# Reordering the first loads, the squares and the warm-up matmuls in the opening of a hybrid attention block

## The chip, the cores and the metric

The kernel runs on one core of one Trainium2 chip. The metric is the device time of one execution in microseconds (us), lower is better; a version's time is the median of its runs.

## The reference

The block normalises `x` (512 tokens of 2048 features, float32), multiplies it with a wide input weight, runs two groups of attention heads on the result, multiplies with an output weight, adds `x` and normalises again. What matters here is only its first step:

```python
y = xf * lax.rsqrt(jnp.mean(xf * xf, axis=-1, keepdims=True) + RMS_EPS)
h = y * norm_g
proj = h @ w_in[l]
```

The rest (rotary positions, compressed, selected and windowed attention of group A, windowed attention with sinks of group B, the gates and the output product) is not touched by the change.

## The kernel before

The kernel holds `x` transposed: 16 tiles of 128 features by 512 tokens, indexed by `k`. Products run in three matmuls of rounded words (`mm3`, lines 118 to 121): every operand is split in a high word (`xh`, `whi`), which is the operand rounded, and a low word (`xl`, `wlo`), which is what is left. Line 119 multiplies high by high, line 120 low `x` by high weight, line 121 high `x` by low weight.

The opening is the loop of lines 178 to 188 over `k`. For each `k` it loads one tile of `x` (`load_x`, 256 KB) and one tile of the first 512 weight columns (`w0`, 256 KB), splits both, and issues 4 times 3 matmuls of 128 x 512 into four accumulators. The division by the root of the mean square is not done here: the loop also sums the squares of `x` over the 16 tiles in `sqa`, and lines 190 to 198 turn the sum into the scale `rstdb` that later results are multiplied with. `norm_g` does enter here. It lies in the small tile `gt` (128 rows of 17 numbers, 8.5 KB), and ScalarE multiplies by a column of it while it rounds:

```python
nc.sync.dma_start(xr, xT[:, k, :])
last["xh"] = act.activation(xh[:, k, :], xr, AF.Copy, scale=gt[:, k:k + 1]).ins
```

So the first `xh` needs both the first tile of `x` and `gt`. VectorE then computes `xl` (`split_x`, line 153), also with `gt`. ScalarE squares the tile (lines 157 and 161), and GpSimd adds the square to `sqa` (line 162). The weights are rounded by ScalarE (line 97) and their rests taken by VectorE (line 99); for the first weight tile VectorE does both (lines 94 and 99).

Loads go through queues, each served in order: SyncE's (SP) has `gt` and then, in turns, tiles of `x` and of weights; ScalarE's (ACT) has only the first weight tile (line 92 with `opening=True`). Tiles of `x` have 5 buffers (`tmp`, line 142), raw weights 3, split weights 3, and the square 1.

Before the loop, `WARM` = 40 matmuls of a 128 x 128 tile of zeros with itself run on TensorE (lines 175 and 176). They produce nothing that is used.

The program is written in a framework that sets the semaphores itself and orders the instructions of each engine by a planner; `tc.issue_after(i)` forces an instruction behind `i` on the same engine.

Of the kernel before, what the change touches and what calls it, by code (L numbers as in the profile page):

```python
# [10 lines left out]
F32 = mybir.dt.float32  # L11
F32R = mybir.dt.float32r
AF = mybir.ActivationFunctionType
# [4 lines left out]
P = 128  # L18
S = 512
# [7 lines left out]
SCALE_B = 64 ** -0.5  # L27
CMP = 32
MOVING, EVEN, STILL, BELOW = 0, 16, 32, 48
WARM = 40  # L30
ORDER = [0, 1, 2, 3, 4, 5, 8, 9, 10, 11, 6, 7, 12, 13, 14, 15]
TAB_W = 512 + NQ * CMP + 256

# [2 lines left out]
def hybrid_block(ctx, tc, xT, xtm, w0, wv0, wv1, wz, wq, wo0, wos, cw1, cw2, cpos, e2, rope, tabs, sinks, gT, fg, out):  # L36
    nc = tc.nc
    pe, act, dve, pool = nc.tensor, nc.scalar, nc.vector, nc.gpsimd

    def sb(name, bufs=1, side=None):  # L40
        return tc.tile_pool(name=name, bufs=bufs, side=side)
# [13 lines left out]
    gt = const.tile([P, KT + 1], F32, name="gt")  # L55
# [13 lines left out]
    last = {}  # L69
# [6 lines left out]
    def raw():  # L76
        raws[0] += 1
        return weights(f"raw{raws[0] % 3}")

    def words(place):  # L80
        return [wp.tile([P, 1088], F32R, name=nm, tag=nm)[:, place:place + 1024] for nm in ("whi", "wlo")]
# [6 lines left out]
    def load_unit(src, width, opening=False, place=EVEN, after=None, after_lo=None, loaded=None):  # L88
        rw = loaded or raw()
        hi, lo = words(place)  # L90
        if loaded is None:
            last["dma"] = (nc.scalar if opening else nc.sync).dma_start(rw[:, :width], src).ins
        if opening:
            dve.tensor_copy(hi[:, :width], rw[:, :width])
        else:
            with tc.issue_after(after) if after else nullcontext():
                last["hi"] = act.activation(hi[:, :width], rw[:, :width], AF.Copy).ins  # L97
        with tc.issue_after(after_lo) if after_lo else nullcontext():
            last["lo"] = dve.tensor_tensor(out=lo[:, :width], in0=rw[:, :width], in1=hi[:, :width].bitcast(F32),  # L99
                                           op=ALU.subtract).ins  # L100
        return hi, lo
# [6 lines left out]
    xh = xpool.tile([P, KT, S], F32R, name="xh")  # L108
# [9 lines left out]
    def mm3(ps, ah, al, bh, bl, first, last, go_on=False):  # L118
        pe.matmul(ps, ah, bh, start=first, stop=False, skip_group_check=go_on)  # L119
        pe.matmul(ps, ah, bl, start=False, stop=False, skip_group_check=go_on)  # L120
        recent["mm"] = pe.matmul(ps, al, bh, start=False, stop=last, skip_group_check=go_on).ins  # L121
# [15 lines left out]
    s0b = p0.enter_context(sb("s0b", bufs=2))  # L137
# [1 line left out]
    ps0 = p0.enter_context(tc.tile_pool(name="ps0", bufs=1, space=PSUM))  # L139

    def tmp(name):
        return s0b.tile([P, S], F32, name=name, tag="tmp", bufs=5)

    def load_x(k):
        xr = tmp("xr")
        if k == 0:
            nc.sync.dma_start(gt, gT)
        nc.sync.dma_start(xr, xT[:, k, :])
        last["xh"] = act.activation(xh[:, k, :], xr, AF.Copy, scale=gt[:, k:k + 1]).ins
        return xr  # L150

    def split_x(k, xr):
        dve.scalar_tensor_tensor(out=xl[:, k, :], in0=xr, scalar=gt[:, k:k + 1], in1=xh[:, k, :].bitcast(F32),
                                 op0=ALU.mult, op1=ALU.subtract)
        if k == 0:
            with tc.issue_after(last["xh"]):
                act.activation(sqa, xr, AF.Square)
        else:
            sq = s0b.tile([P, S], F32, name="sq", tag="sq", bufs=1)
            with tc.issue_after(last["xh"]):  # L160
                act.activation(sq, xr, AF.Square)
            pool.tensor_tensor(out=sqa, in0=sqa, in1=sq, op=ALU.add)

    def bank(i):
        if i >= 6:
            return psp.tile([P, 512], F32, name="pj", tag="pj")
        return ps0.tile([P, 512], F32, name=f"bank{i}", tag=f"bank{i}")

    sqa = s0.tile([P, S], F32, name="sqa", tag="sqa")
# [4 lines left out]
    idle = bank(0)  # L174
    for i in range(WARM):
        pe.matmul(idle[:, 0:P], still, still, start=True, stop=True)
    acc0 = [bank(i) for i in (4, 2, 5, 3)]
    for k in range(KT):
        if k == 0:
            hi, lo = load_unit(w0[:, 0, 0:512], 512, opening=True)  # L180
            xr = load_x(k)
        else:
            xr = load_x(k)
            hi, lo = load_unit(w0[:, k // 2, (k % 2) * 512:(k % 2) * 512 + 512], 512)
        split_x(k, xr)
        for i in range(4):
            o = i * P
            mm3(acc0[i], hi[:, o:o + P], lo[:, o:o + P], xh[:, k, :], xl[:, k, :], k == 0, k == KT - 1)
# [220 lines left out]
    def rows(m):  # L409
        if m < 6:  # L410
            xr = rb.tile([P, 2, S], F32, name="rows", tag="rows")
        else:
            xr = wk.tile([P, 2, S], F32, name="rows", tag="raw3", bufs=1)
        with tc.issue_after(last["dma"]):
            nc.sync.dma_start(xr, xT[:, 2 * m:2 * m + 2, :])
        return xr
# [46 lines left out]
    xr = None  # L463
    for i in range(8):
# [4 lines left out]
        if 0 < i < 7:  # L469
            xr = rows(i - 1)  # L470
# [346 lines left out]
    xr = rows(6)  # L817
# [11 lines left out]
    for u in range(4):  # L829
# [10 lines left out]
        if u == 0:  # L840
            build(6, xr)
            xr = rows(7)
# [308 lines left out]
    for c, u, ms in ((0, 0, ()), (0, 1, ()), (0, 2, ()), (1, 0, (0, 1, 2)), (1, 1, (3, 4)), (1, 2, (5, 6)), (0, 3, ()),  # L1151
                     (1, 3, (7,))):
        hi, lo = load_unit(wo0[:, c, u], 1024, place=MOVING, loaded=first_units.pop(0) if first_units else None, after=last["qh"],
                           after_lo=low_y[11] if (c, u) == (0, 2) else last["turn"])
# [365 lines left out]
```

## Time and profile before

| what | value |
|---|---|
| time, median of 3 runs | 802.83 us (802.57 to 803.43) |
| time of the profiled execution | 802.8 us |
| its span, first to last instruction | 801.0 us |
| TensorE (PE) busy | 789.6 us, 99% of the span |
| VectorE (DVE) busy | 686.3 us, 86% |
| ScalarE (ACT) busy | 504.7 us, 63% |
| GpSimd (POOL) busy | 108.3 us, 14% |
| granted TensorE clock, mean | 0.997 |

A profile shows one execution. PE is the row of matmuls, PEld that of their weight loads. Matmuls overlap, and the end of one is modelled, so the step from one start to the next is the real pace. "ACTq" and "SPq" are the queues that issue transfers.

### The profile page before, as it was taken

What the parts mean: (1) busy time and instruction counts of PE and PEld (TensorE: products, weight loads), DVE (VectorE), ACT (ScalarE), POOL (GpSimd) and SP (SyncE); (2) the same over time, 40 slices, a digit from 0 to 9 for tenths busy, and PEclk for the clock granted to TensorE, in tenths of its full rate; (3) what the DMA queues carried; (4) which work ended last, traced back from release to release, by engine and by line L of the source; (5) the groups of instructions that cost most, each with busy time, mean ns of one, the idle gap of its engine ahead of it and who ended that gap; (6) DMA issues with size and microseconds to landing.
All of it is one profiled execution on the core that took longest, in us unless ns stands there. A gap on an engine that the chain in (4) does not pass through costs nothing.

```text
span 801.0 us, 15316 instructions
## 1 busy us (share of the span) xinstructions
PE 789.6 (99%) x5693; PEld 739.1 (92%) x5693; DVE 686.3 (86%) x1407; ACT 504.7 (63%) x1103; POOL 108.3 (14%) x111
## 2 busy tenths in 40 slices
PE   9999999999999999999999999999999999999996
PEld 8788888888888899999999999999999999999996
DVE  7668988889989597759999999998999798978895
ACT  6646657655666356664447778777777867553545
POOL 3615002110121000323210110110100000000000
PEclk9999999999999999999999999999999999999998
DMA  7572243564373469887723213225216836797845
GB/s 239 172 242 81 79 144 106 171 171 150 101 210 106 158 200 281 257 269 194 207 82 106 68 53 119 82 92 159 71 50 216 296 120 219 257 266 193 258 86 211
DMA packets 49563, 131.05 MB, mean 164 GB/s; under 512 B 6000, under 2 KB 8848, under 8 KB 49488
## 3 DMA queue, kind: packets, MB, share of 16 engines
q1 hardware_dynamic: 43376, 110.89, 42.3%
q0 software_dynamic: 5824, 18.65, 10.5%
q8 instruction: 45, 0.74, 0.4%
q10 hardware_dynamic: 288, 0.52, 0.2%
q14 instruction: 30, 0.25, 0.1%
HBM read 113.23 MB, written 16.81 MB: 162 GB/s over the span
## 4 chain that ended last, share of the span: by engine, by line
PE 86%; DVE 6%; DMA 3%; ACT 2%; issue 2%; POOL 0%; SPq 0%; DVEq 0%; ACTq 0%
PE pj L119 16%; PE pj L121 15%; PE pj L120 15%; PE oa L120 5%; PE oa L119 5%; PE oa L121 5%; PE sp L932 4%; PE bank L121 2%; PE bank L120 2%; PE bank L119 2%; DMA xr<-xT 2%; DVE wlo L543 2%; PE tp L969 2%; PE tp L384 2%; DMA raw<-wq 1%
## 5 line engine op out<-in xcount | busy, mean ns | idle before, releaser
L119 PE MATMUL pj<-xh,whi 128*128 128x256 f32 (+1 forms) x592 | 196.9, 333 | 0.6 <-ACT t L608 0.5
L121 PE MATMUL pj<-xh,wlo 128*128 128x256 f32 (+1 forms) x592 | 196.2, 331 | 0.0
L120 PE MATMUL pj<-xl,whi 128*128 128x256 f32 (+1 forms) x592 | 196.1, 331 | 0.0
L119 PEld LDWEIGHTS pj<-xh,whi 128*128 128x128 f32 x592 | 111.4, 188 | 11.0 <-ACT t L608 0.9
L121 PEld LDWEIGHTS pj<-xh,wlo 128*128 128x128 f32 x592 | 111.4, 188 | 10.1
L120 PEld LDWEIGHTS pj<-xl,whi 128*128 128x128 f32 x592 | 111.4, 188 | 9.7
L543 DVE TENSOR_TENSOR wlo<-raw,whi 128x1024 fp32r<-128x1024 f32 (+2 forms) x80 | 92.9, 1172 | 7.8 <-ACT whi L542 7.2
L542 ACT ACTIVATE whi<-raw 128x1024 fp32r<-128x1024 f32 (+2 forms) x80 | 77.6, 985 | 30.7 <-DVE raw L581 11.5
L99 DVE TENSOR_TENSOR wlo<-raw,whi 128x1024 fp32r<-128x1024 f32 (+1 forms) x61 | 72.1, 1184 | 22.8 <-ACT whi L97 22.3
L97 ACT ACTIVATE whi<-raw 128x1024 fp32r<-128x1024 f32 (+1 forms) x60 | 56.6, 945 | 28.8 <-PE pj L120 14.8
L120 PE MATMUL oa<-wlo,xh 128*128 128x256 f32 x200 | 55.5, 278 | 0.0
L119 PE MATMUL oa<-whi,xh 128*128 128x256 f32 x200 | 55.4, 278 | 0.0
L121 PE MATMUL oa<-whi,xl 128*128 128x256 f32 x200 | 55.2, 276 | 0.0
L121 PE MATMUL pj<-pu,wlo 128*128 128x256 f32 x160 | 45.0, 281 | 0.5 <-DVE wlo L543 0.5
L119 PE MATMUL pj<-pu,whi 128*128 128x256 f32 x160 | 45.1, 282 | 0.4 <-DVE zr L581 0.4
L120 PE MATMUL pj<-pu,whi 128*128 128x256 f32 x160 | 44.7, 279 | 0.0
L289 DVE TENSOR_TENSOR pl<-tp,ph 128x512 fp32r<-128x512 f32 (+1 forms) x64 | 40.7, 651 | 3.1 <-ACT ph L288 2.9
L288 ACT ACTIVATE ph<-tp 128x512 fp32r<-128x512 f32 (+1 forms) x64 | 34.1, 560 | 9.6 <-PE tp L969 4.4
L363 ACT ACTIVATE ttb<-ttb,sums 128x256 f32<-128x256 f32 (+1 forms) x64 | 30.0, 471 | 14.4 <-DVE sums L356 14.4
L121 PEld LDWEIGHTS oa<-whi,xl 128*128 128x128 f32 x200 | 37.6, 188 | 0.0
L120 PEld LDWEIGHTS oa<-wlo,xh 128*128 128x128 f32 x200 | 37.6, 188 | 0.0
L119 PEld LDWEIGHTS oa<-whi,xh 128*128 128x128 f32 x200 | 37.5, 188 | 0.0
(401 smaller groups left out, 2369.8 us busy)
## 6 DMA issues: line engine op xcount, KB each, us to landing
raw<-wq SPq DMA_DIRECT2D x41, 512.0 KB, 4.4
raw<-wz SPq DMA_DIRECT2D x36, 512.0 KB, 4.0
cw<-cw SPq DMA_DIRECT2D x32, 256.0 KB, 4.0
raw<-wos SPq DMA_DIRECT2D x14, 512.0 KB, 5.9
rw<-wos SPq DMA_DIRECT2D x10, 512.0 KB, 4.8
xr<-xT SPq DMA_DIRECT2D x16, 256.0 KB, 3.4
rows<-xT SPq DMA_DIRECT2D x8, 512.0 KB, 4.7
raw<-wo SPq DMA_DIRECT2D x8, 512.0 KB, 6.0
```

The costliest lines, as they stand in the source:

```text
L97: last["hi"] = act.activation(hi[:, :width], rw[:, :width], AF.Copy).ins
L99: last["lo"] = dve.tensor_tensor(out=lo[:, :width], in0=rw[:, :width], in1=hi[:, :width].bitcast(F32), op=ALU.subtract).ins
L119: pe.matmul(ps, ah, bh, start=first, stop=False, skip_group_check=go_on)
L120: pe.matmul(ps, ah, bl, start=False, stop=False, skip_group_check=go_on)
L121: recent["mm"] = pe.matmul(ps, al, bh, start=False, stop=last, skip_group_check=go_on).ins
L288: act.activation(ph, tp, AF.Copy)
L289: dve.tensor_tensor(out=pl, in0=tp, in1=ph.bitcast(F32), op=ALU.subtract)
L363: act.activation(tv, tv, AF.Exp, bias=mn[:, e, v:v + 1], scale=-1.0, accum_out=dn[:, e, v:v + 1])
L384: pe.transpose(tp[:, o:o + P], tts[kt + s][:, v, c0:c0 + P], ident)
L542: split_hi = act.activation(hi, src, AF.Copy).ins
L543: last["lo"] = dve.tensor_tensor(out=lo, in0=src, in1=hi.bitcast(F32), op=ALU.subtract).ins
L932: pe.matmul(sp[:, a:b], qq[:, qs], kk[:, ko:ko + b - a], start=pi == 0, stop=pi == 2)
```

## The change

It touches the opening alone. `gt` leaves SP's queue and is issued on ACT's queue, behind the first weight tile; so the first tile of `x` is the first entry of SP's queue. The square and its addition leave `split_x` for a function of their own, `add_square`; the squares of tiles 0, 1 and 2 are issued later, in the turns of `k` = 2 and 3 (tile 0 at 2; 1 and 2 at 3; 3 and 4 at 4; from 5 on each in its own turn), and behind a rounding of weights on ACT. The square has two buffers and the tiles of `x` six. The matmuls on zeros are 33, where there were 40.

```diff
-WARM = 40
+WARM = 33
...
-        return s0b.tile([P, S], F32, name=name, tag="tmp", bufs=5)
+        return s0b.tile([P, S], F32, name=name, tag="tmp", bufs=6)
 
     def load_x(k):
         xr = tmp("xr")
-        if k == 0:
-            nc.sync.dma_start(gt, gT)
         nc.sync.dma_start(xr, xT[:, k, :])
         last["xh"] = act.activation(xh[:, k, :], xr, AF.Copy, scale=gt[:, k:k + 1]).ins
         return xr
...
-        if k == 0:
-            with tc.issue_after(last["xh"]):
-                act.activation(sqa, xr, AF.Square)
-        else:
-            sq = s0b.tile([P, S], F32, name="sq", tag="sq", bufs=1)
-            with tc.issue_after(last["xh"]):
-                act.activation(sq, xr, AF.Square)
+
+    def add_square(k, xr):
+        sq = sqa if k == 0 else s0b.tile([P, S], F32, name="sq", tag="sq", bufs=2)
+        with tc.issue_after(last["xh"]), tc.issue_after(last["hi"]) if k < 3 else nullcontext():
+            act.activation(sq, xr, AF.Square)
+        if k:
             pool.tensor_tensor(out=sqa, in0=sqa, in1=sq, op=ALU.add)
...
+    behind = []
     for k in range(KT):
         if k == 0:
             hi, lo = load_unit(w0[:, 0, 0:512], 512, opening=True)
+            nc.scalar.dma_start(gt, gT)
             xr = load_x(k)
         else:
             xr = load_x(k)
             hi, lo = load_unit(w0[:, k // 2, (k % 2) * 512:(k % 2) * 512 + 512], 512)
         split_x(k, xr)
+        behind.append((k, xr))
+        for late in range(k >= 2 and min(len(behind), 1 + (k > 2))):
+            add_square(*behind.pop(0))
```

## Rows read from the trace of the kernel before

**Rows 1.** Busy time by engine: us, share, instructions.

```profile
PE 789.6 (99%) x5693; PEld 739.1 (92%) x5693; DVE 686.3 (86%) x1407; ACT 504.7 (63%) x1103; POOL 108.3 (14%) x111
```

**Rows 2.** What PE waited for: total us, times, longest.

```profile
PE bank L176 <- DVE still L173: 1.2, 1, 1.2
PE tp L457 <- issue: 0.6, 1, 0.6
```

**Rows 3.** PE in order of time, opening: start, us, instruction.

```profile
1.16 4.07 PE L176 MATMUL bank<-still 128*128 128x128 bf16 x40 [1.16 <-DVE still L173]
5.09 1.19 PE L119 MATMUL bank<-xh,whi 128*128 128x512 f32 x4
6.12 0.39 PE L120 MATMUL bank<-xl,whi 128*128 128x512 f32 x1
```

**Rows 4.** Stretches, matmuls on zeros: length, busy (x running), clock, DMA, GB/s.

```profile
2.42:3.49 1.07, 1.07 (x13) 1.00 0.99 346
...
4.70:5.00 0.30, 0.30 (x8) 1.00 0.97 335
```

**Rows 5.** ACT and its queue in order of time, opening.

```profile
0.73 0.40 ACTq L92 DMA_DIRECT2D raw<-w  x1
1.17 1.28 ACT L67 ACT_TABLE_LOAD   x1 [1.17 <-PEq L1511]
...
4.32 0.72 ACT L149 ACTIVATE xh<-xr,gt 128x512 fp32r<-128x512 f32 x1 [1.65 <-DMA xr<-xT]
...
6.89 0.62 ACT L97 ACTIVATE whi<-raw 128x512 fp32r<-128x512 f32 x1
```

**Rows 6.** DVE in order of time, around the first `xl`.

```profile
5.07 0.75 DVE L153 SCALAR_TENSOR_TENSOR xl<-xr,gt,xh 128x512 fp32r<-128x512 f32 x1 [0.33 <-ACT xh L149]
```

**Rows 7.** SP's queue in order of time, opening.

```profile
0.74 0.38 SPq L147 DMA_DIRECT2D gt<-gT  x1
1.17 0.89 SPq L148 DMA_DIRECT2D xr<-xT  x2
```

**Rows 8.** First transfers: queue, size, us from issue to landing.

```profile
raw<-w ACTq DMA_DIRECT2D x1, 256.0 KB, 2.8
gt<-gT SPq DMA_DIRECT2D x1, 8.5 KB, 2.5
...
xr<-xT SPq DMA_DIRECT2D x1, 256.0 KB, 3.1
```

**Rows 9.** Packets by queue from 2.3 to 2.6 us (q10 ACT's, q1 SP's): packets, MB, share.

```profile
q10 hardware_dynamic: 39, 0.08, 87.5%
q1 hardware_dynamic: 34, 0.00, 7.8%
```

**Rows 10.** One stretch, all engines: busy (x running), clock, DMA share, GB/s.

```profile
6.00:7.00 1.00, 1.00 (x6) 0.82 (x5) 0.50 (x1) 1.00 (x3) 0.00 (x0) 1.00 1.06 385
```

**Rows 11.** PE in order of time, 35 to 37 us.

```profile
35.63 0.39 PE L119 MATMUL bank<-xh,whi 128*128 128x512 f32 x1
36.33 0.50 PE L121 MATMUL bank<-xh,wlo 128*128 128x512 f32 x1 [0.31 <-DVE wlo L99]
36.67 0.40 PE L120 MATMUL bank<-xl,whi 128*128 128x512 f32 x1
```

**Rows 12.** ACT in order of time, 31 to 36 us.

```profile
32.35 0.72 ACT L149 ACTIVATE xh<-xr,gt 128x512 fp32r<-128x512 f32 x1 [0.16 <-DMA xr<-xT]
33.72 0.63 ACT L161 ACTIVATE sq<-xr 128x512 f32<-128x512 f32 x1 [0.64 <-POOL sqa L162]
34.26 0.61 ACT L97 ACTIVATE whi<-raw 128x512 fp32r<-128x512 f32 x1
```

**Rows 13.** DVE in order of time, the same stretch.

```profile
34.90 1.38 DVE L99 TENSOR_TENSOR wlo<-raw,whi 128x512 fp32r<-128x512 f32 x1 [0.67 <-ACT whi L97]
```

**Rows 14.** The last addition on POOL.

```profile
42.90 1.29 POOL L162 TENSOR_TENSOR sqa<-sqa,sq 128x512 f32<-128x512 f32 x1 [0.74 <-ACT sq L161]
```

**Rows 15.** PE's first use of the sum.

```profile
49.43 1.02 PE L191 MATMUL bank<-sqa,ones 128*128 128x512 f32 x2
```

**Rows 16.** Stretches at the end, all engines: columns as in Rows 10.

```profile
793.00:795.00 2.00, 0.45 (x4) 0.25 (x3) 0.62 (x3) 0.80 (x3) 0.00 (x0) 1.00 0.60 226
...
796.00:797.00 1.00, 0.00 (x0) 0.00 (x0) 0.21 (x1) 0.40 (x1) 0.00 (x0) 0.79 0.58 217
```

## The prediction

> **What bounds the kernel now.** I read the busy table first, then what PE waited for, then the opening engine by engine, and last the packets of its first transfers. The busy table leaves one candidate: PE works 789.6 of 801.0 us [rows 1]. The reader should see in the list of PE's waits how little is left: 1.2 us before its first instruction, and nothing else above 0.6 us [rows 2]. After the last matmul the span has only some 7.6 us of tail, from 793.45 on [rows 16]. So a microsecond by which the first real matmul moves passes through to the end nearly whole, and nothing that the change does on another engine counts unless PE gets its operands earlier or later for it. The change can therefore be priced at two places: where the real matmuls start, and where PE stands still inside the opening loop.
>
> The start. The matmuls on zeros run from 1.16 us, the first real matmul starts at 5.09 [rows 3]. In a stretch of 1.07 us there are 13 of the small ones, three of them overlapping neighbours of the stretch: one per 107 ns, which is 128 columns at 1.2 GHz; at 4.70 to 5.00 the pace is 56 ns, which is 2.4 GHz [rows 4]. The clock column reads 1.00 in both, so in this opening the spacing has to be read, not the column. The rise lies near 4.69 us, after 3.5 us of unbroken work. Forty in this pace end at 5.07. The first `xh` is ready at 4.32 + 0.72 = 5.04 [rows 5]. PE starts 0.05 later. Both conditions are met almost together: shortening the warm-up alone, or hastening `xh` alone, would give nothing.
>
> What makes `xh` late is its wait for the tile of `x`, which lands at 1.17 + 3.1 = 4.27 [rows 7, 8]; `gt` was there at 0.74 + 2.5 = 3.24.
>
> The standstill. At 35.63 a matmul starts, the next at 36.33, the one after at 36.67 [rows 11]. The undisturbed step is (6.12 - 5.09) / 4 = 0.26 at worst [rows 3], and 0.23 in the rows just ahead; so the place costs 0.70 + 0.34 - 2 x 0.23 = 0.58 us. Its releaser is `wlo`, and behind that a square: ACT's square waited 0.64 us for POOL to free its one buffer, the rounding of weights stood behind it on ACT until 34.26, and DVE took 1.38 us for the rest, to 36.28 [rows 12, 13].
>
> **The change part by part.**
>
> *Matmuls on zeros, 40 to 33.* The seven that go are the last ones, at 56 ns: 0.4 us. Thirty-three end at 1.16 + 33 x 0.107 = 4.69. PE is free from there; this is worth something only if `xh` comes before 5.04. By itself: 0.
>
> *x's first tile leads SP's queue.* It is issued at 0.74, not at 1.17: 0.43 us earlier [rows 7]. Whether it lands earlier depends on the transfer engines, which all queues share. Before, three transfers passed first: weights and `x` of 256 KB each and the 8.5 KB of `gt`, the last landing at 4.27. The two big ones still have to pass together, and both are needed for the first matmul (`whi` comes of the weights). Sixteen engines at 385 GB/s [rows 10] pass a row of 2 KB in 85 ns; 128 rows of each make 8 rows an engine. Taking away `gt`'s 8 short rows, about 12 ns each by their share in [rows 9] (7.8% of 16 engines x 0.3 us over 34 packets = 11 ns), saves 0.1 us: `x` and the first weights land at about 4.17. The weights land later than their 0.73 + 2.8 = 3.53 of before [rows 5, 8], since they now alternate with `x`, but still before `xh` is needed. The optimistic bound is the whole 0.43 us, `x` at 3.84.
>
> *gt behind the first weights.* This is where I expect the cost. `gt` now stands behind the weights in ACT's queue, and while it passes, SP's queue offers the second tile of `x`. How the engines share two queues is shown by the same two transfers of before: from 2.3 to 2.6 us, 39 packets of 2 KB of one queue and 34 short ones of the other passed [rows 9], so they take turns row by row. That is why 8.5 KB took 2.5 us to land beside 256 KB that took 2.8 [rows 8]. After the change, 8 rows of `gt` and its closing packet each wait for one row of 85 ns of `x`'s second tile: 9 x 85 + 8 x 12 = 0.86 us after 4.17, so `gt` lands at about 5.03. Then `xh` from 5.08 to 5.80, first matmul at about 5.85: 0.76 us later than before. The lower bound, if the short rows pass in one go, is 4.17 + 0.1 = 4.27, as `x` before: 0. I take 0.75, since rows 9 show exactly such a pair.
>
> The Trainium skill (DMA: Bandwidth & Descriptors, Queues, rings and completion order) says that an engine goes round the queues packet by packet and drains a whole packet of many descriptors, typically 9 to 17, before it switches. By that the eight rows of `gt` would pass in one turn and the sum would lose its 0.75; the counts of [rows 9] speak against it, one short packet for one long one.
>
> The issue itself costs ACT about 0.40 us, like the one at 0.73 [rows 5]; the table load behind it then ends near 2.85, not 2.45, and ACT is idle until `x` lands. Cost 0.
>
> *First L120.* `xl` takes 0.75 us behind `xh` [rows 6], and is needed 1.03 us after the first matmul [rows 3]: unchanged relative to the start, 0.
>
> *Squares of tiles 0 to 2 later, two buffers, six tiles of x.* Two squares of 0.54 us each (33.72 to 34.26, [rows 12]) leave ACT ahead of the rounding at 6.89, which ends at 7.51 [rows 5]. PE needs that for the second tile, twelve matmuls after its start: 5.09 + 1.03 + 8 x 0.23 = 7.96. It was in time already: 0. What counts is the second buffer: the square at 33.72 no longer waits 0.64 us, so `wlo` is there near 35.64 and the 0.58 us standstill goes. A start 0.75 later would by itself give the same slack: the two don't add. I take -0.58; the bound on the other side is 0, if another wait on DVE takes its place. The delayed squares need their additions on POOL done before PE reads the sum at 49.43; the last ended at 44.19 [rows 14, 15], a cover of 5.2 us. The delay is at the front, where POOL has time between turns: 15 additions of about 1.3 us are 20 us of work in a loop of 44: 0. If that cover went, PE would wait there for what is missing of it.
>
> *Sum.* +0.75 - 0.58 = +0.2 us (rounded) on the profiled execution's 802.8, which stands 0.03 below the median of its runs: 803.0. Bounds: start -0.43 to +0.76, standstill -0.58 to 0.
>
> **The rivals.**
>
> A, forecast: `gt` is the late operand and the standstill goes: 803.0, between 802.6 and 803.6 with the bound of the standstill.
>
> B: `gt` passes in one go; `xh` starts as before, the standstill goes: 802.8 - 0.6 = 802.2. For it: the page's rule. Against: rows 9.
>
> C, faster: `x` lands its whole 0.43 earlier with `gt` beside it. The first matmul comes at 4.66, just where 33 warm-up matmuls end: 802.8 - 0.43 - 0.58 = 801.8. For it: the fit with 33. Against: transfers that fill the engines, 385 GB/s a few us on. It decides if `xh` starts before 4.0.
>
> D, slower: the clock. In A, PE is idle from 4.69 to 5.85, around the moment at which it rose. If the rise is put off, the real matmuls run at 1.2 GHz, half pace. Let it need as much work again as before, 3.5 us from 5.85: half of it is lost, 1.75 us, giving 804.8. Against: at the end PE finishes at 793.45 and the clock column still averages 0.79 in 796 to 797, so it fell only near 796.6, after 3.1 us of rest [rows 16]; a gap of 1.2 need not do harm. For: rest before the rise is not shown by any row. It decides if the first real matmuls step by 0.43 us instead of 0.23.
>
> E: the planner orders instructions far behind the opening otherwise. No row speaks for a sign; either way, up to 2 us.
>
> **How the numbers follow.** A 0.50, B 0.24, C 0.07, D 0.13, E 0.06. From no change a measurement can tell about 0.2%, 1.6 us here: below 801.2 is faster, above 804.4 slower. A, B and C all lie inside. Slower is most of D and half of E with a little of A's tail, 0.15; faster is half of E and a little of C, 0.05; the same 0.80. The range takes A, B and C with the spread of runs, 801.7 to 804.2, and leaves out D and E.
>
> **What would show it.** In the profile after: `xr` landing near 4.2 and `gt` near 5.0; ACT's first `xh` waiting for `gt` and starting near 5.1; the first L119 near 5.85 and PE idle for about 1.1 us before it; no gap at the twelfth tile; squares that no longer wait for POOL for long; L191 about 0.2 us later than 49.43. I am wrong if `xh` starts by 4.4 (then B or C), if the first real matmuls step at half pace (D), or if PE's list of waits has a new entry above 0.5 us behind the opening (E).

## The result, and the profile after

The changed kernel takes 807.82 us (median of 11 runs), the kernel before 803.16 (11 runs beside them): a ratio of 1.0056, 95% interval 1.0042 to 1.0070, some 4.5 us slower. The forecast was 803.0 with a range of 801.7 to 804.2. The profiled execution took 808.47 us with a span of 806.7. One run of the kernel before, timed beside the experiments (983.27 us at a mean granted clock of 0.752), is in the slow state and left out of every ratio.

TensorE's list of waits now has two entries ahead of all others; its columns are those of [rows 2]. Lines 147, 151, 157, 159 and 173 of the changed kernel are lines 149, 153, 161, 162 and 176 of before.

```profile
PE bank L121 <- DVE wlo L99: 2.7, 3, 1.8
PE bank L119 <- ACT xh L147: 1.9, 1, 1.9
PE bank L173 <- DVE still L170: 1.2, 1, 1.2
```

The second entry is the start. PE in order of time, answering to [rows 3]:

```profile
1.16 3.31 PE L173 MATMUL bank<-still 128*128 128x128 bf16 x33 [1.16 <-DVE still L170]
6.36 1.30 PE L119 MATMUL bank<-xh,whi 128*128 128x512 f32 x4 [1.88 <-ACT xh L147]
7.46 0.63 PE L120 MATMUL bank<-xl,whi 128*128 128x512 f32 x1
...
8.31 0.63 PE L120 MATMUL bank<-xl,whi 128*128 128x512 f32 x1
8.74 0.63 PE L121 MATMUL bank<-xh,wlo 128*128 128x512 f32 x1
```

The first real matmul starts at 6.36, 1.27 us later than before, and from 7.46 on the step is 0.43 us: half pace. Why it starts late stands on ACT and its queue, answering to [rows 5], and in the first transfers, answering to [rows 8]:

```profile
1.23 0.39 ACTq L179 DMA_DIRECT2D gt<-gT  x1
2.46 0.20 ACT L67 ACTIVATE small<-small 128x1 f32<-128x1 f32 x1
5.58 1.33 ACT L147 ACTIVATE xh<-xr,gt 128x512 fp32r<-128x512 f32 x2 [2.92 <-DMA gt<-gT]
```

```profile
raw<-w ACTq DMA_DIRECT2D x1, 256.0 KB, 4.0
gt<-gT ACTq DMA_DIRECT2D x1, 8.5 KB, 4.3
...
xr<-xT SPq DMA_DIRECT2D x1, 256.0 KB, 3.8
```

ACT waits for `gt`, which lands at 1.23 + 4.3 = 5.5; the tile of `x` was there at 0.74 + 3.8 = 4.5 although it led its queue, 0.3 us later than the 4.27 of before. The packets from 4.2 to 4.8 us show `gt` (q10) among the tiles of `x` that follow the first (q1): 116 short packets beside 119, of which some 107 are rows of 2 KB (0.22 MB). Columns are as in [rows 9]:

```profile
q1 hardware_dynamic: 119, 0.22, 94.0%
q10 hardware_dynamic: 116, 0.01, 14.0%
```

The half pace is in the clock column this time (stretches of 1 us; columns as in [rows 10], the clock third from the end):

```profile
6.00:7.00 1.00, 0.64 (x3) 0.54 (x4) 0.66 (x1) 1.00 (x3) 0.00 (x0) 1.00 1.02 375
7.00:8.00 1.00, 1.00 (x5) 0.76 (x4) 1.00 (x3) 1.00 (x3) 0.00 (x0) 0.67 1.07 412
8.00:9.00 1.00, 1.00 (x4) 0.81 (x3) 1.00 (x3) 1.00 (x4) 0.00 (x0) 0.50 1.05 388
...
10.00:11.00 1.00, 1.00 (x4) 0.84 (x3) 1.00 (x2) 0.64 (x2) 0.00 (x0) 0.63 0.91 297
11.00:12.00 1.00, 1.00 (x6) 0.78 (x6) 0.80 (x2) 1.00 (x3) 0.08 (x1) 1.00 0.95 330
```

A mean of 0.67 in the second row puts the fall at 7.34, one of 0.63 in the fourth the rise at 10.74: 3.4 us in which a matmul steps by 0.43 and not 0.23, a loss of 3.4 x (1 - 0.227 / 0.427) = 1.6 us.

The first entry of the list is the larger surprise. The place answering to [rows 11], the largest of three:

```profile
33.87 0.39 PE L120 MATMUL bank<-xl,whi 128*128 128x512 f32 x1
36.09 0.73 PE L121 MATMUL bank<-xh,wlo 128*128 128x512 f32 x2 [1.84 <-DVE wlo L99]
```

The three cost 3.5 us together (steps of 0.65, 2.23 and 0.99 and the longer step of 0.335 behind each, less six of 0.227); before there was one of 0.58. VectorE and GpSimd around it, answering to [rows 13, 14]:

```profile
29.18 1.78 DVE L99 TENSOR_TENSOR wlo<-raw,whi 128x512 fp32r<-128x512 f32 x1
30.88 3.48 DVE L151 SCALAR_TENSOR_TENSOR xl<-xr,gt,xh 128x512 fp32r<-128x512 f32 x2
34.29 1.75 DVE L99 TENSOR_TENSOR wlo<-raw,whi 128x512 fp32r<-128x512 f32 x1
```

```profile
23.54 8.57 POOL L159 TENSOR_TENSOR sqa<-sqa,sq 128x512 f32<-128x512 f32 x5 [1.19 <-ACT sq L157]
32.46 4.73 POOL L159 TENSOR_TENSOR sqa<-sqa,sq 128x512 f32<-128x512 f32 x3 [0.35 <-ACT sq L157]
```

GpSimd adds without a pause, five additions in 8.57 us, and every VectorE operation beside it takes 1.75 us or so. The rounding of weights was done near 33.4; its `wlo` starts only at 34.29, behind two `xl`.

So the profile's 5.7 us are: start +1.27; half pace +1.6; standstills 3.5 - 0.58 = +2.9; together 5.8. PE's first use of the sum is at 55.28 (49.43 in [rows 15]), 5.85 later, and in this execution nothing more is lost behind the opening.

### The profile page after: what moved, and what is told of

It reads as the page before. It is cut to its first block, busy times and chain, and to the rows that moved or that the text cites. A ratio compares the mean times of both kernels' runs of the same rounds, so it can differ in the third digit from the quotient of the medians.

```text
span 806.7 us, 15317 instructions
## 1 busy us (share of the span) xinstructions
PE 791.9 (98%) x5686; PEld 739.6 (92%) x5686; DVE 690.5 (86%) x1407; ACT 505.0 (63%) x1103; POOL 110.7 (14%) x111
## 4 chain that ended last, share of the span: by engine, by line
PE 84%; DVE 8%; DMA 4%; issue 2%; ACT 2%; ACTq 0%; SPq 0%; DVEq 0%
PE pj L119 15%; PE pj L121 15%; PE pj L120 15%; PE oa L120 5%; PE oa L121 5%; PE oa L119 5%; PE sp L934 4%; PE bank L120 3%; PE bank L119 3%; PE bank L121 3%; PE tp L971 2%; DVE wlo L545 1%; PE tp L386 1%; DVE wlo L99 1%; DMA raw<-wq 1%
```

## The experiments

All were timed in five rounds beside the kernel before. Ratios are to before, with 95% intervals. "Start" is the first real matmul, "loop" the time from it to the first use of the sum; both are from PE's order of time in one profile each.

| kernel | ratio | interval | start us | loop us |
|---|---|---|---|---|
| before | 1 | | 5.09 | 44.34 |
| the change | 1.0056 | 1.0042 to 1.0070 | 6.36 | 48.92 |
| e1 gt alone | 1.0013 | 1.0001 to 1.0025 | 6.30 | 44.30 |
| e2 squares and buffers alone | 1.0056 | 1.0040 to 1.0071 | 5.39 | 49.81 |
| e3 change, gt put back | 1.0038 | 1.0025 to 1.0052 | 5.29 | 48.26 |
| e4 change, 60 on zeros | 1.0076 | 1.0060 to 1.0092 | 6.99 | 47.43 |
| e5 second square buffer alone | 1.0045 | 1.0029 to 1.0061 | 5.23 | 48.26 |
| e6 late squares alone | 1.0009 | 0.9996 to 1.0023 | 5.36 | 43.65 |
| e7 six buffers for x alone | 0.9999 | 0.9985 to 1.0013 | 5.37 | 44.26 |
| e8 as e2, additions on VectorE | 0.9989 | 0.9977 to 1.0000 | 5.37 | 43.72 |
| e9 change, additions on VectorE | 1.0005 | 0.9993 to 1.0018 | 6.39 | 45.26 |
| e10 as e9, gt second on SP | 0.9994 | 0.9980 to 1.0008 | 5.61 | 43.68 |
| e11 change, one square buffer | 1.0003 | 0.9991 to 1.0015 | 6.39 | 46.48 |
| e12 before, additions on VectorE | 1.0001 | 0.9987 to 1.0015 | 5.37 | 43.78 |

A profile is one execution. Behind the first use of the sum every version has the same matmuls, and yet this stretch took 751.6 us in the profile of before, 750.3 in that of e9 and 754.8 in that of e7. What a part costs is therefore read from the ratios, and that the parts of the change's profile add up to its span within 0.1 us is luck in part. Against the times expected, the medians of e2, e5, e10 and e12 came out 0.6 to 1.4 us above their ranges and that of e6 0.1 above; e3 came 1.0 us under e2, where 0.5 was allowed; e4 fell into its rival's range.

**e1: gt behind the first weights, nothing else.**

```diff
-        if k == 0:
-            nc.sync.dma_start(gt, gT)
...
             hi, lo = load_unit(w0[:, 0, 0:512], 512, opening=True)
+            nc.scalar.dma_start(gt, gT)
```

> The kernel before with one part of the change: gt leaves SP's queue and goes behind the first weights on ACT's; 40 matmuls on zeros, squares as before. Theory: the later landing of gt is the whole cause of the late start: gt lands near 5.5 us, first L119 at 6.3 to 6.4 us (5.09 before), the 40 matmuls on zeros end at 5.0 or, if the clock rises early, sooner, PE rests over 1 us, and the clock may or may not fall behind it; no standstill of more than 0.6 us near the twelfth tile. Time 0.8 to 2.5 us over before, 803.9 to 805.7. Rival: the squares carry most of the loss: then this is within 1 us of before.

The first real matmul starts at 6.30, and the loop is as long as before. ACT in order of time:

```profile
5.52 0.72 ACT L147 ACTIVATE xh<-xr,gt 128x512 fp32r<-128x512 f32 x1 [2.86 <-DMA gt<-gT]
```

The late start is wholly `gt`'s; its price is 0.13%, 1.0 us. The rest of 1.2 us before the first matmul did not bring the clock down in this profile. The time is also within the rival's 1 us: most of the loss lies elsewhere.

**e2: the squares and buffers, nothing else** (the changed kernel with `gt` as before and 40 matmuls on zeros).

> The kernel before with the other part: squares of tiles 0 to 2 later, two buffers for the square, six for the tiles of x; gt at the head of SP's queue, 40 matmuls on zeros. Theory: two thirds of the loss of the change's profile lie in its standstills on wlo (some 3.5 us in all, 0.58 before), and they come of the squares and buffers: first L119 at 5.1, but steps of 1 to 2 us on wlo from the tenth tile on: 805 to 806. Rival: the standstills follow from the late start and the fallen clock: then no standstill, 802.4 to 802.8.

This is the full ratio of the change, 1.0056, without the move of `gt`; with e1's 0.13% the two parts make 0.69%, which the intervals allow. The start, 5.39, is the end of the 40 small matmuls, which ran at the slow pace for longer here; the loop is 5.5 us longer. Its largest standstill, PE in order of time, and the clock behind it:

```profile
32.88 0.39 PE L119 MATMUL bank<-xh,whi 128*128 128x512 f32 x1
35.33 0.73 PE L121 MATMUL bank<-xh,wlo 128*128 128x512 f32 x2 [2.07 <-DVE wlo L99]
```

```profile
33.00:36.00 3.00, 0.93 (x5) 0.58 (x4) 3.00 (x3) 2.03 (x4) 2.84 (x3) 1.00 0.00 0
36.00:37.00 1.00, 1.00 (x5) 0.81 (x4) 1.00 (x2) 0.55 (x1) 0.92 (x2) 0.68 0.67 117
37.00:39.00 2.00, 1.97 (x5) 1.05 (x5) 2.00 (x2) 0.71 (x2) 1.92 (x2) 0.50 0.19 73
```

A standstill inside the loop can be followed by a fall of the clock as the rest ahead of it was: a mean of 0.68 puts the fall at 36.36, 1 us after PE went on. The mean granted clock of each run says how often this came: five of e2's six runs have 0.995, as this profile, while the runs of the kernel before that count have 0.997 to 0.999.

**e3: the changed kernel with gt put back** to the head of SP's queue, 33 matmuls on zeros.

> The changed kernel with gt alone put back to the head of SP's queue; 33 matmuls on zeros, squares later, two and six buffers. Theory that gt makes the start late: first L119 at 5.1, PE rests 0.3 to 0.6 us before it, the clock does not fall, and what is left are the standstills: as e2 within 0.5 us. Rival, 33 are too few by themselves: the clock still rises late or falls, over 1 us slower than e2.

The first real matmul starts at 5.29, the list of waits has 3.0 us of standstills on `wlo`, and the clock does not fall in this profile. Two of its five runs have a mean clock of 0.995, fewer than e2's. Its interval overlaps e2's, so 33 or 40 matmuls can't be told apart by time.

**e4: the changed kernel with a longer warm-up.**

```diff
-WARM = 33
+WARM = 60
```

> The changed kernel with 60 matmuls on zeros in place of 33, so that PE works nearly until xh is there at 6.3 us. Theory: the rest of 2 us before the first real matmul is what lets the clock fall at 7.3 in the profile; without the rest the real matmuls step by 0.23 us from the start, and 1 to 1.7 us come back against the changed kernel: 806 to 807. Rival: the fall is independent of the rest: steps of 0.43 us for some microseconds here too, and the time of the changed kernel, 807.8 or more.

This missed in time: 809.37 us is what the rival said. In the steps it went as the theory had it, with none of 0.43 us among the real matmuls. But the clock rose late in this profile, near 6.4, so the sixty ran at the slow pace until then and pushed the start to 6.99, and the standstills stayed (2.9 us in the list of waits). Here covering the rest with work went with no fall of the clock, and cost more at the start than that gave back.

**e5: a second buffer for the square, nothing else.**

```diff
-            sq = s0b.tile([P, S], F32, name="sq", tag="sq", bufs=1)
+            sq = s0b.tile([P, S], F32, name="sq", tag="sq", bufs=2)
```

> The kernel before with a second buffer for the square, nothing else. Theory: with one buffer GpSimd's additions were paced by the square, which waited for the buffer, and VectorE got its turns in the pauses; with two the additions run back to back, and each VectorE operation beside them takes 1.7 to 1.8 us where it took 0.7 (as in e2). Two such per tile of x are 3.5 us, over the 2.72 us that TensorE needs for a tile: standstills on wlo of 1.5 us or more in all (0.58 before), most VectorE operations between 20 and 40 us at 1.7, time 804.5 to 806. Rival, the late squares or the sixth tile buffer are the cause: no more than 0.6 us of standstill, 802.6 to 803.2.

This one digit gives 0.45% of the 0.56. VectorE from 28 to 39 us, then GpSimd:

```profile
27.59 0.74 DVE L153 SCALAR_TENSOR_TENSOR xl<-xr,gt,xh 128x512 fp32r<-128x512 f32 x1
28.25 0.68 DVE L99 TENSOR_TENSOR wlo<-raw,whi 128x512 fp32r<-128x512 f32 x1
29.05 3.30 DVE L153 SCALAR_TENSOR_TENSOR xl<-xr,gt,xh 128x512 fp32r<-128x512 f32 x2
32.27 1.78 DVE L99 TENSOR_TENSOR wlo<-raw,whi 128x512 fp32r<-128x512 f32 x1
33.98 1.77 DVE L153 SCALAR_TENSOR_TENSOR xl<-xr,gt,xh 128x512 fp32r<-128x512 f32 x1
```

```profile
28.54 10.04 POOL L162 TENSOR_TENSOR sqa<-sqa,sq 128x512 f32<-128x512 f32 x6 [1.43 <-ACT sq L161]
```

The first two operations start while GpSimd is idle: 0.74 and 0.68 us. From 28.54 GpSimd adds six times without a pause, 1.67 us each, and VectorE's operations go to 1.65 to 1.78: they take turns with the additions. Two such operations for a tile are 3.5 us; PE needs 12 x 0.227 = 2.72 for a tile.

**e6 and e7: the two other parts of the squares, each alone** (late squares with one buffer and five tiles; six buffers for `x` in the kernel before).

> The kernel before with the squares of tiles 0 to 2 later, one buffer for the square, five for the tiles of x. Theory of the second buffer: within 0.8 us of before, standstills under 1 us. Rival, the squares that are late pile the additions up: standstills of 2 us and more, 805 or over.

> The kernel before with six buffers for the tiles of x in place of five. Theory of the second square buffer: within 0.8 us of before. Rival: with a sixth buffer the tiles of x go ahead of the weights in SP's queue, and the last weights come too late: standstills on wlo of 2 us and more behind 30 us, whose wlo waits for whi and whi for a DMA, 805 or over.

Neither can be told from before, and neither profile has a standstill in the loop, not even the 0.58 us of before. Together with e5 they account for e2 within the intervals: 0.45 + 0.09 - 0.01 = 0.53%.

**e8: e2 with the additions on VectorE.**

```diff
-            pool.tensor_tensor(out=sqa, in0=sqa, in1=sq, op=ALU.add)
+            dve.tensor_tensor(out=sqa, in0=sqa, in1=sq, op=ALU.add)
```

> e2 (late squares, two and six buffers, gt at the head of SP's queue, 40 matmuls on zeros) with the 15 additions on VectorE in place of GpSimd. Theory that additions on GpSimd stretch VectorE's operations: every VectorE operation at 0.7 us, three per tile of x are 2.1 us, under 2.72; no standstill on wlo above 0.3 us: 802.2 to 803.0, level with before or up to 0.6 us under it. Rival, the order of loads or of xl and wlo is the cause: standstills of over 1 us here too, 805 or over.

With the same squares, buffers and loads as e2, no standstill is left; from 0.9989 against 1.0056 the additions on GpSimd cost e2 0.67%, some 5 us. VectorE from 20 to 35 us, grouped by line (x count, busy us, mean ns, idle):

```profile
L161 DVE TENSOR_TENSOR sqa<-sqa,sq 128x512 f32<-128x512 f32 x8 | 5.5, 688 | 0.3
L99 DVE TENSOR_TENSOR wlo<-raw,whi 128x512 fp32r<-128x512 f32 x7 | 4.8, 684 | 0.0
L153 DVE SCALAR_TENSOR_TENSOR xl<-xr,gt,xh 128x512 fp32r<-128x512 f32 x6 | 4.4, 748 | 2.0 <-ACT xh L149 2.0
```

and the same stretch of the changed kernel:

```profile
L151 DVE SCALAR_TENSOR_TENSOR xl<-xr,gt,xh 128x512 fp32r<-128x512 f32 x7 | 11.2, 1632 | 0.0
L99 DVE TENSOR_TENSOR wlo<-raw,whi 128x512 fp32r<-128x512 f32 x4 | 6.0, 1496 | 0.0
```

VectorE did 21 operations where it had done 11, in the same 15 us, and had time left. (Neighbours overlap a little at their ends, so the busy times add up to more than the stretch.)

**e9, e10: the changed kernel with the additions on VectorE (the same line as in e8), and with gt second in SP's queue on top.**

```diff
         nc.sync.dma_start(xr, xT[:, k, :])
+        if k == 0:
+            nc.sync.dma_start(gt, gT)
...
-            nc.scalar.dma_start(gt, gT)
```

> The changed kernel, all its parts, with the 15 additions on VectorE in place of GpSimd. Theory: two separate losses; this takes away the standstills on wlo (none above 0.4 us) and leaves the late gt: first L119 at 6.2 to 6.5 us, a rest of 1.5 to 2 us before it, and in some executions the clock falls behind that rest: 803.2 to 805. Rival, the standstills need the late start too: over 805.

> As e9, with gt second in SP's queue, behind the first tile of x and ahead of the second. Theory that gt was late because its short rows took turns with 2 KB rows of another queue: ACT's queue is empty by then, gt passes at once behind x's first tile, and the first L119 comes at 4.9 to 5.4, set by the two big first transfers that share the engines, not 0.43 earlier than the 5.09 of before: 802.0 to 803.0. Rival, any place behind the big transfers makes gt late: 6 us or more.

In e9 the standstills are gone, the first real matmul starts at 6.39, and in its profile the clock fell near 7.67 behind a rest of 2 us. In e10 ACT waited for `gt` until 4.84, not 5.5; its start of 5.61 missed the expectation of 5.4 at most, but the rival's 6 us by more. `gt` lands 0.4 us behind `x` (1.17 + 3.6 against 0.74 + 3.6), where it was 1.0 behind. The reason expected does not hold as it stands, for ACT's queue was not empty by then. Packets from 3.5 to 4.0 us, columns as in [rows 9]:

```profile
q1 hardware_dynamic: 169, 0.09, 60.6%
q10 hardware_dynamic: 57, 0.09, 47.7%
```

While `gt` passed on q1 (most of the 169 packets are short: 0.09 MB are some 44 rows of 2 KB), the first weights still passed on q10, so its short rows shared the engines here too. What the move shows is that `gt` need not be as late as behind the weights. x's place at the head still bought nothing: it lands at 4.3.

**e11: the changed kernel with one buffer for the square.**

> The changed kernel with one buffer for the square in place of two, additions on GpSimd. Theory: the additions are paced again and the standstills on wlo shrink to 1 us or less in all; what is left is the late gt: 803.8 to 805.5. Rival, the second buffer only counts with the rest unchanged: 806.5 or over.

GpSimd's additions, from the same part of the loop:

```profile
31.07 1.42 POOL L159 TENSOR_TENSOR sqa<-sqa,sq 128x512 f32<-128x512 f32 x1 [1.13 <-ACT sq L157]
33.23 1.56 POOL L159 TENSOR_TENSOR sqa<-sqa,sq 128x512 f32<-128x512 f32 x1 [0.74 <-ACT sq L157]
35.54 1.29 POOL L159 TENSOR_TENSOR sqa<-sqa,sq 128x512 f32<-128x512 f32 x1 [0.74 <-ACT sq L157]
```

The pauses of 0.74 us and more are back, no standstill on `wlo` is in the list of waits, and the ratio falls from 1.0056 to 1.0003; the median, 803.86, is at the lower end of what was expected. Its loop of 46.48 is long because PE stepped at half pace from 6.4 to 12.5 us: behind the rest the clock came up late.

**e12: the kernel before with the additions on VectorE.**

> The kernel before with the 15 additions on VectorE, nothing else. Theory: the 0.58 us standstill near 36 us goes, the start stays: 802.2 to 803.0, under before by less than what can be told from it. Rival: VectorE, now with three operations per tile, becomes late itself: new standstills, 803.8 or over.

The standstill of [rows 11] is gone and the loop 0.56 us shorter, as the theory has it, though e6 and e7 lost that standstill with the additions on GpSimd. The ratio is 1.0001: against a spread of 802 to 806 us such a gain does not show. Besides, the time of its runs is 2.2 to 2.35 us above their spans, where this difference is 1.7 to 1.9 us for the kernel before; it is 1.9 to 2.7 for e8 to e10 as well, so some of what additions on VectorE give inside the span is lost outside it. No run asked why. No version beats the kernel before clearly; e8 comes nearest.

## Why the prediction was wrong, point by point

**What bounds the kernel** held: PE alone, and what the opening loses passes through.

**The squares and two buffers** are the step that failed. I wrote: "the square at 33.72 no longer waits 0.64 us, so `wlo` is there near 35.64 and the 0.58 us standstill goes", and took -0.58 with 0 as the other bound. In its place the change's profile has 2.9 us more of standstills; e5 shows +0.45% (3.6 us) for the second buffer alone, e11 the way back. Two readings were wrong. The wait of the square for GpSimd was taken for a loss; it was what made GpSimd pause, and VectorE ran freely only in these pauses. And the 1.38 us of `wlo` in [rows 13] were taken for the length of the operation. It was already one stretched by the addition beside it, and the trace of before has both lengths:

```profile
31.85 0.69 DVE L99 TENSOR_TENSOR wlo<-raw,whi 128x512 fp32r<-128x512 f32 x1
34.43 1.30 POOL L162 TENSOR_TENSOR sqa<-sqa,sq 128x512 f32<-128x512 f32 x1 [0.74 <-ACT sq L161]
```

The first starts while GpSimd rests, from 31.13 to 32.27. The second is the addition that runs beside the `wlo` of [rows 13]. In e8 the mean is 0.68. Where the sum says that 15 additions have time enough on GpSimd, it asks whether GpSimd is in time, not who works slower while it works. So neither the sum nor a rival had a loss there at all.

The Trainium skill (SBUF — State Buffer, Who interferes with whom) states the rule that the step needed: a VectorE instruction with two inputs in SBUF contends with a GpSimd instruction that reads SBUF, and the port pair that the two share is an exclusive lock. `xl`, `wlo` and the additions are all of this kind. The traces agree in the main: a VectorE operation took 0.68 to 0.75 us alone and 1.65 to 1.78 in turns with additions of 1.67. They do not show a lock for the whole of both: alone, an operation and an addition (1.29 in [rows 14]) would make 2.0 us, and a pair in turns took 1.7.

**gt behind the first weights** held in its mechanism and was too small in size: +0.76 was forecast for the start, +1.27 came (e1: +1.21). The price of the turns was right: from the landing of the weights ahead of it (0.73 + 4.0 = 4.7) to its own at 5.5 are 0.8 us, where 0.86 was forecast. What was mis-sized is where they begin: I let the two big transfers land at 4.17, and they landed at 4.5 (`x`) and 4.7. Packets of the changed kernel up to 4.2 us:

```profile
q1 hardware_dynamic: 209, 0.39, 32.7%
q10 hardware_dynamic: 158, 0.26, 22.9%
```

The two queues had moved 0.65 MB, against 0.68 before, but 0.13 MB of q1's are beyond the first tile of `x`: rows of the second tile passed before the first had landed. That they are what delayed it is likely and not shown. The rule of the Trainium skill that rival B rested on, by which a queue's many short rows pass in one turn, did not hold here, neither before nor after: 34 short packets beside 39 long ones in [rows 9], and 116 beside some 107. The turns are not strict throughout, though: from 1.8 to 2.3 us of the kernel before, 63 packets of q1 passed beside 26 of q10. The issue of `gt` cost ACT nothing, as forecast, though the table load did not slip to 2.85 either: what follows it started at 2.46.

**x's first tile leads its queue**: costed at 0.1 us of gain, came as 0.3 of loss. Rival C did not come: the tile was issued 0.43 us earlier and landed later, with no more data moved by 4.2 us than before.

**Rival D**, the clock, came true in the profile, in another form: it rose early, then fell behind a rest of 2.1 us, 1 us after work had gone on. Its 1.75 us were 1.6. In the argument against it I relied on the 3.1 us of rest at the end of the program [rows 16]; rests of 2 us turned out to be enough at times. It is the smaller part of the ratio: the clock does not fall in the profiles of e3 and e5, which are 0.38% and 0.45% slower. By the mean clock of each run, 3 of the change's 11 runs (0.994 or 0.995) had such a fall; at 1.6 us each that is an estimated 0.4 us of its 4.5, and 1.3 us of e2's loss with five of six.

**Seven fewer on zeros** did nothing by itself that could be measured (e2 and e3 differ in it, and their intervals overlap).

## What to carry to other kernels

Before a wait is taken away, ask what the waiting engine holds back: an engine off the critical path that is paced by a scarce buffer may be the reason that the engine on it runs at full speed. When one instruction has two durations in a trace (here 0.7 and 1.4 us), find out what runs beside the long one before either is used as a price. And a small transfer can cost by its rows and by what shares the engines with it, more than by its bytes: here 8.5 KB in 128 rows took 2.5 us to land from the head of a queue and 4.3 from behind a big one.

## What the runs showed of the hardware

The clock fell after shorter rests than the end of the program suggested. Of seven places in the openings of these profiles where PE went from one start to the next in 1.8 to 2.5 us, three were followed by a fall 1.0 to 1.3 us after work had resumed (the change at 4.3 us, e9, e2), one by a late rise (e11), and three by nothing (the change at 33.9, e5, e3). Of nine steps of 1.0 to 1.6 us (one each in e1, e2, e3 and e10, two in e5, three in e4), none was.

The moment of the first rise, too, differs from profile to profile with the same start of work at 1.16 us: from near 4 us (the change, e10) to 5.6 (e2, e12), 6.4 (e4) and 6.6 (e7). With 40 matmuls on zeros a late rise sets the start (5.36 to 5.39 in five profiles), where in the profile of before the last of them and the first `xh` came within 0.03 us of each other. These moments are read from the steps between PE's matmuls, since the column of the granted clock reads 1.00 ahead of its first record.
